# Two mixed layers in one kernel: attention released by its first block of queries instead of by the end of the projections

## The chip, the cores and the metric

The kernel runs on one core of a Trainium2 chip. The metric is device microseconds of one execution, a median over runs. One profiled execution of the kernel before is read here; it gives busy time, waits and the granted clock of every engine. TensorE (PE in the rows) does the matmuls, VectorE (DVE) and ScalarE (ACT) read their results and prepare operands, GpSimd (POOL) takes a part of the elementwise work, and SyncE (SP) issues nearly all transfers.

## The reference, cut to what matters

The program is two blocks, one after the other, over 512 positions of 1024 features, with 256 more positions of context in the first. The change touches only the two layers of the first block. In each of them one projection of the normalised input feeds three mixers, whose outputs are joined and projected back:

```python
ux = hx @ w_in[l]                      # 18 column blocks of 128
uc = hc @ (w_in[l] if ctx_out else w_in[l][:, OFF_K:OFF_HQ])
fx = fourier_mix(col(ux, OFF_FOURIER, FOURIER_W), w_four[l])
ax, ac = attention_group(ux, uc, base_c, q_norm[l], k_norm[l], tabs, ctx_out)
rx, rc = hgrn_group(ux, uc, base_c, lb_all[:, l], hg_norm[l], ctx_out)
x = x + g_a * (jnp.concatenate([fx, ax, rx], axis=-1) @ w_out[l])

def attend(q, k, v):                   # 8 heads, 2 of keys and values
    s = jnp.einsum('bkgqd,bksd->bkgqs', q, k).astype(jnp.float32) * (HEAD_DIM ** -0.5)
    p = jax.nn.softmax(s, axis=-1).astype(v.dtype)
    return jnp.einsum('bkgqs,bksd->bkgqd', p, v)
```

`hgrn_group` is a gated linear recurrence in both directions (four heads, handled as two pairs). In layer 0 context and positions both need outputs (768 columns); in layer 1 only the 512 positions do, though keys, values and the recurrence still read the context.

## The kernel before

All products of weights and activations are made of three float32r products (high by high, high by low, low by high; `mm3`, lines 245 to 247). So each weight block is fetched by a transfer on SP's queue (line 229), rounded to its high half on ACT (line 230), and its low half is made by a subtraction on DVE or POOL (line 232) before PE can use both.

Memory is handed out by two allocators written in the kernel, one for plain float32 (`arena`) and one for rounded operands (`rarena`, 440 units of 64 floats in each partition). A request takes room that was freed longest ago in a zone for short-lived buffers; a request marked long takes the lowest free room. A buffer's next owner waits for the last reader of the one before. A further 152 units (`room`) are lent to the plain allocator during the mixers.

A layer's mixers are class `Mix1`. Its work is written as generators that yield an estimated cost after each piece, and `_weave` (line 117) always continues the generator that is furthest behind, so the order of the code follows these costs. A scheduler then orders each engine's queue from that code. The generators are:

- `dense` (line 731): the projections, in the order values of the recurrence (2 blocks), its output gate (2), keys (1), attention values (1), queries (4, one block of 128 columns is two heads), Fourier inputs (2), and for the second pair of recurrence heads two gates and the queries. It ends by setting the flags `in1` and `dense`.
- `hgrn(0)` and `hgrn(1)` (line 826): the recurrence of a pair of heads. The first can start at once, the second when `in1` is set. Per step it makes state tiles `sn` (line 905).
- `attention` (line 962): for each of the four query blocks `j` and its two heads, scores (line 992), a row softmax over 768 keys (lines 562 to 571, with the exponential on ACT, line 568), the transposition of the normalised probabilities by a matmul with a diagonal (line 1004), their split into two halves (lines 212 and 213), and the product with the values (lines 1008 and 1009). It begins when `dense` is set.
- `fourier` (line 1022): also begins when `dense` is set; it follows `hgrn(1)` in its chain.
- in layer 0, `mod_cols`: products for later modulation vectors (line 498 on DVE, with a transfer of `w_ada` for each).

The gates of the recurrence use ACT's sigmoid (`zgate`, lines 640 and 641); attention uses its exponential. After the mixers come the output projection and the next phase (first additions at line 1107).

## Time and profile before

| | |
|---|---|
| median of 3 runs | 3878.45 us (3872.4 to 3878.79) |
| profiled execution, its own time | 3877.54 us |
| span of its profile | 3875.8 us |
| PE busy over the span | 3704.2 us, 96% |
| mean granted TensorE clock | 0.976 |
| layer 0: from the first query block's end to the last projection | 190 to 264 us |
| layer 0: attention | 264 to 510 us |
| layer 1: the same two stretches | 1266 to 1324 us, and 1324 to 1500 us |

A line on waits gives who waited, for whom, the total, the number of waits and the longest. A line on windows gives, for a stretch, the busy time of each engine (a union of its instructions) with the number of instructions in brackets. PE's busy time holds matmuls that overlap in the pipeline, so a share of 100% is not the peak rate, but a share below it is time in which PE had nothing running. The clock column is 1.00 at 2.4 GHz and 0.50 at 1.2 GHz, averaged over the stretch.

### The profile page before, as it was taken

The numbers are of one execution on the slowest core, as the hardware profiler recorded it, in microseconds if no ns is written. First come the engines' busy times: TensorE is split into PE (matmuls) and PEld (weight loads), VectorE is DVE, ScalarE is ACT, GpSimd is POOL, SyncE is SP. The second block draws the span as 40 slices with busy tenths as digits, with TensorE's granted clock in tenths as the row PEclk, the third lists the DMA queues.
The fourth block names the chain that finished last, engine by engine and source line by source line (L and its number), as shares of the span: only waits on it lengthen the run. The fifth ranks groups of instructions, "written<-read, shape, count | busy, mean of one in ns | idle before, by whom it ended". The sixth has DMA issues, their size and how long they took to land. (4 is left out here: it accounts for less than half of the span.)

```text
span 3875.8 us, 50567 instructions
## 1 busy us (share of the span) xinstructions
PE 3704.2 (96%) x20474; PEld 3203.6 (83%) x20474; DVE 1975.8 (51%) x3638; ACT 1345.3 (35%) x2263; POOL 591.6 (15%) x539
## 2 busy tenths in 40 slices
PE   6998899999999988999999998999999999999998
PEld 5776788888887778888988896798888888888887
DVE  8687756443254666333542358653236333736233
ACT  4233544431232354322332335443223222324222
POOL 3331012540013421000100021020002000211001
PEclk8998999999998999999999999999999999999999
DMA  5222115452202112322122321123222222312222
GB/s 208 66 93 67 39 40 181 144 181 92 61 33 74 39 65 71 103 94 91 66 95 92 110 75 51 55 90 102 81 98 98 98 75 95 109 66 98 98 94 75
DMA packets 95834, 345.12 MB, mean 89 GB/s; under 512 B 10864, under 2 KB 14064, under 8 KB 95600
## 3 DMA queue, kind: packets, MB, share of 16 engines
q1 hardware_dynamic: 95024, 341.37, 26.6%
q8 instruction: 160, 2.62, 0.3%
q14 instruction: 74, 0.61, 0.0%
q10 hardware_dynamic: 576, 0.52, 0.0%
HBM read 334.51 MB, written 4.19 MB: 87 GB/s over the span
## 5 line engine op out<-in xcount | busy, mean ns | idle before, releaser
L245 PE MATMUL psum<-rarena,room 128*128 128x512 f32 (+1 forms) x3121 | 1092.9, 351 | 5.1 <-ACT rarena L212 2.6
L247 PE MATMUL psum<-rarena,room 128*128 128x512 f32 (+1 forms) x3053 | 1076.4, 353 | 0.8 <-DVE room L232 0.8
L246 PE MATMUL psum<-rarena,room 128*128 128x512 f32 (+1 forms) x3065 | 1074.9, 351 | 0.5 <-DVE rarena L213 0.5
L247 PE MATMUL psum<-rarena 128*128 128x512 f32 (+1 forms) x2108 | 744.7, 354 | 9.9 <-DVE rarena L232 9.5
L245 PE MATMUL psum<-rarena 128*128 128x512 f32 (+1 forms) x2040 | 735.1, 361 | 16.2 <-ACT rarena L212 5.8
L246 PE MATMUL psum<-rarena 128*128 128x512 f32 (+1 forms) x2008 | 720.0, 359 | 1.3 <-DVE rarena L213 1.3
L245 PEld LDWEIGHTS psum<-rarena,room 128*128 128x128 f32 x3121 | 592.8, 190 | 82.5 <-ACT rarena L212 3.0
L246 PEld LDWEIGHTS psum<-rarena,room 128*128 128x128 f32 x3065 | 582.4, 190 | 76.0 <-DVE rarena L213 0.8
L247 PEld LDWEIGHTS psum<-rarena,room 128*128 128x128 f32 x3053 | 580.0, 190 | 78.7 <-DVE room L232 1.0
L232 DVE TENSOR_TENSOR room<-arena,room 128x1024 fp32r<-128x1024 f32 (+2 forms) x250 | 325.3, 1306 | 531.9 <-PE psum L246 231.5
L230 ACT ACTIVATE room<-arena 128x1024 fp32r<-128x1024 f32 (+2 forms) x290 | 320.1, 1110 | 738.0 <-DMA arena<-gu 242.1
L299 POOL TENSOR_TENSOR arena<-arena 128x256 f32<-128x256 f32 x170 | 136.5, 810 | 2282.8 <-ACT arena L297 2212.9
L247 PEld LDWEIGHTS psum<-rarena 128*128 128x128 f32 x2108 | 403.1, 191 | 64.2 <-DVE rarena L232 10.4
L245 PEld LDWEIGHTS psum<-rarena 128*128 128x128 f32 x2040 | 391.6, 192 | 75.5 <-ACT rarena L230 6.9
L246 PEld LDWEIGHTS psum<-rarena 128*128 128x128 f32 x2008 | 385.7, 192 | 54.6 <-DVE rarena L213 1.7
L230 ACT ACTIVATE rarena<-arena 128x1024 fp32r<-128x1024 f32 (+2 forms) x138 | 154.7, 1122 | 334.3 <-DMA arena<-gu 123.6
L232 DVE TENSOR_TENSOR rarena<-arena,rarena 128x1024 fp32r<-128x1024 f32 (+2 forms) x98 | 131.4, 1342 | 235.5 <-ACT rarena L230 114.9
L212 ACT ACTIVATE rarena<-arena 128x512 fp32r<-128x512 f32 (+2 forms) x257 | 131.2, 528 | 206.2 <-DVE arena L410 179.5
L213 DVE TENSOR_TENSOR rarena<-arena,rarena 128x512 fp32r<-128x512 f32 (+1 forms) x246 | 149.3, 622 | 87.9 <-ACT rarena L212 87.6
L297 ACT ACTIVATE arena<-arena 128x256 f32<-128x256 f32 (+1 forms) x274 | 106.9, 412 | 239.2 <-DVE arena L1230 117.3
L410 DVE TENSOR_TENSOR arena<-arena,psum 128x512 f32<-128x512 f32 (+1 forms) x170 | 100.5, 598 | 157.2 <-PE psum L247 150.9
L500 POOL TENSOR_TENSOR arena<-arena 128x1024 f32<-128x1024 f32 x48 | 125.4, 2619 | 199.9 <-DMA arena<-w_ada 88.9
(391 smaller groups left out, 4327.8 us busy)
## 6 DMA issues: line engine op xcount, KB each, us to landing
arena<-gu SPq DMA_DIRECT2D x264, 512.0 KB, 3.7
arena<-dn SPq DMA_DIRECT2D x80, 704.0 KB, 4.1
arena<-w_ada SPq DMA_DIRECT2D x60, 512.0 KB, 3.4
room<-w_ada SPq DMA_DIRECT2D x36, 512.0 KB, 4.0
room<-w_in SPq DMA_DIRECT2D x30, 512.0 KB, 3.3
arena<-c_in SPq DMA_DIRECT2D x24, 512.0 KB, 3.2
arena<-dn SPq DMA_DIRECT2D x16, 448.0 KB, 3.4
room<-ab_in SPq DMA_DIRECT2D x14, 512.0 KB, 3.2
```

Of the source, the lines that this page charges most:

```text
L212: A.activation(h, src, AF.Copy)
L213: eng.tensor_tensor(lo, src, h.bitcast(F32), ALU.subtract)
L230: A.activation(h.r, r.f, AF.Copy)
L232: (G if wlo[1] < wlo[0] else V).tensor_tensor(lo.r, r.f, h.f, ALU.subtract)
L245: PE.matmul(ps, h[:, s], ah, start=k == 0, stop=False)
L246: PE.matmul(ps, h[:, s], al_, start=False, stop=False)
L247: PE.matmul(ps, lo[:, s], ah, start=False, stop=k == nk - 1)
L297: A.activation(sq.f, src, AF.Square)
L299: (V if self.fast else G).tensor_tensor(self.parts[0].f, self.parts[0].f, sq.f, ALU.add)
L410: V.tensor_tensor(s.f, s.f, pu, ALU.mult)
L500: G.tensor_tensor(t.f, r.f, sic[q].f, ALU.mult)
```

## The change

Each query block sets a flag of its own in `dense` as soon as it has been projected, normalised and rotated. `attention` starts when the first query block's flag is set (`FIRSTQ` names block 0 for both layers), and at each further block waits for that block's flag. Nothing is computed that was not computed before. The state tiles of the recurrence become long allocations, that is, they are taken from the low end of the plain memory and no longer from the zone for short-lived buffers.

```diff
                     self.qf.append(qf)
                     self.rq.append(r8)
+                    flags.add(f"q{j}")
                     yield costq
...
-                        sn = al(128)
+                        sn = al(128, True)
                         G.memset(sn.f, 0.0)
...
-                while "dense" not in flags:
+                while f"q{FIRSTQ[l]}" not in flags:
                     yield None
...
                 for j in range(4):
+                    while f"q{j}" not in flags:
+                        yield None
                     ao = al(W, True)
...
+FIRSTQ = (0, 0)
```

By the costs that the generators yield, attention now runs from the end of the first query block. In layer 0 it has done 2.3 of its four blocks when `dense` ends, and the rest beside `hgrn(1)` and `fourier`; before, it did 2.1 blocks beside those two and 1.9 alone. In layer 1 it has done 2.3 blocks at the end of `dense` and the rest beside `hgrn(1)`; `fourier`, which had attention beside it, comes after it, and one block that attention did alone at the end is no longer there.

How that stands in the queues is shown at two places. Line numbers of the changed file are one higher after line 804 and three higher in `attention`: scores are L995 there, the transposition L1007, the products with the values L1011 and L1012. The first place is PE's queue in layer 0 where the query blocks are projected. Before, the three products of a block follow each other with only the small sums of squares (L727) between:

```order
L247 MATMUL psum<-rarena 128x512
L245 MATMUL psum<-rarena 128x512
L246 MATMUL psum<-rarena 128x512
L247 MATMUL psum<-rarena 128x512
L245 MATMUL psum<-rarena 128x512
L246 MATMUL psum<-rarena 128x512
L727 MATMUL psum<-hs,room 128x2 x2
L247 MATMUL psum<-rarena 128x512
```

Now, between the second and third query block, the first head's transpositions, value products and the next scores stand in it:

```order
L1007 MATMUL psum<-arena,room 128x128
L1007 MATMUL psum<-room 128x128 x2
L727 MATMUL psum<-hs,room 128x2 x4
L1011 MATMUL psum<-rarena 128x512
L1007 MATMUL psum<-room 128x128
L1007 MATMUL psum<-arena,room 128x128
L1007 MATMUL psum<-room 128x128 x2
L1012 MATMUL psum<-rarena 128x512
L1011 MATMUL psum<-rarena 128x512
L995 MATMUL psum<-rarena 128x256 x2
```

What moved is attention's work, from behind the last projection to between the projections.

The second place is ACT's queue in layer 1, at the gates of the second pair of recurrence heads. Before, the sigmoids stand together, and the one load of a function table before the first exponential comes after them:

```order
L641 ACTIVATE arena<-psum 128x256
L640 ACTIVATE arena<-psum 128x512
L641 ACTIVATE arena<-psum 128x512
L976 ACTIVATE rarena<-arena 64x512 x2
L854 ACTIVATE room<-arena 128x256
L819 ACTIVATE arena<-psum 128x512
L854 ACTIVATE room<-arena 128x128x2 x2
L866 ACTIVATE room<-psum 128x512
L568 ACT_TABLE_LOAD
```

Now exponentials stand between them, and so does the rounding of the next weight block (L230):

```order
L230 ACTIVATE rarena<-room 128x1024
L577 ACTIVATE arena<-psum 64x512
L568 ACT_TABLE_LOAD
L568 ACTIVATE room<-psum,room,arena 128x768 x2
L855 ACTIVATE arena<-arena 128x256
L640 ACT_TABLE_LOAD
L640 ACTIVATE arena<-psum 128x256
L641 ACTIVATE arena<-psum 128x256
L568 ACT_TABLE_LOAD
L568 ACTIVATE room<-psum,room,arena 128x768 x2
L640 ACT_TABLE_LOAD
```

In the whole program the table loads at L640 go from 2 to 7 and those at L568 from 3 to 8.

## Rows read from the trace of the kernel before

**Rows 1.** The page: busy time and share of each engine, and PE's busy tenths by slice.
```profile
PE 3704.2 (96%) x20474; PEld 3203.6 (83%) x20474; DVE 1975.8 (51%) x3638; ACT 1345.3 (35%) x2263; POOL 591.6 (15%) x539
PE   6998899999999988999999998999999999999998
```

**Rows 2.** Windows: length, then busy us (instructions) of five engines, clock, DMA share, GB/s.
```profile
190.00:264.00 74.00, 68.72 (x405) 60.89 (x406) 58.02 (x127) 20.48 (x36) 22.17 (x12) 0.96 0.32 110
264.00:380.00 116.00, 93.31 (x590) 76.32 (x588) 92.56 (x212) 50.48 (x108) 30.86 (x29) 0.90 0.19 58
430.00:512.00 82.00, 70.57 (x443) 59.77 (x442) 58.57 (x137) 49.13 (x97) 4.31 (x3) 1.00 0.16 49
1266.00:1324.00 58.00, 53.62 (x264) 44.86 (x263) 37.56 (x90) 17.82 (x29) 23.04 (x18) 0.94 0.14 47
1324.00:1410.00 86.00, 76.23 (x468) 63.55 (x467) 56.74 (x120) 41.22 (x86) 31.06 (x42) 0.90 0.08 26
1410.00:1460.00 50.00, 46.84 (x276) 40.03 (x275) 36.24 (x75) 29.59 (x52) 8.70 (x9) 1.00 0.28 91
1460.00:1505.00 45.00, 38.76 (x214) 33.08 (x213) 26.86 (x49) 24.46 (x41) 4.84 (x8) 0.92 0.22 70
2400.00:2550.00 150.00, 140.96 (x764) 115.04 (x762) 96.40 (x265) 68.94 (x159) 19.19 (x20) 0.97 0.19 62
```

**Rows 3.** Timelines (start, us): first query block rotated; last projection, then attention's first instruction.
```profile
190.34 1.26 POOL L549 TENSOR_TENSOR arena<-room 128x512 f32<-128x512 f32 x1 [2.82 <-DVE arena L275]
263.98 0.39 ACT L819 ACTIVATE arena<-psum 128x256 f32<-128x256 f32 x1 [1.18 <-PE psum L247]
264.45 3.46 ACT L976 ACTIVATE rarena<-arena 64x768 fp32r<-64x768 f32 x4
...
1266.37 1.30 POOL L549 TENSOR_TENSOR arena<-room 128x512 f32<-128x512 f32 x1
1324.54 0.60 ACT L819 ACTIVATE arena<-psum 128x512 f32<-128x512 f32 x1 [2.72 <-PE psum L247]
```

**Rows 4.** PE's waits in 430 to 512 us: total, times, longest.
```profile
PE psum L992 <- DVE arena L578: 3.9, 4, 1.6
PE psum L1004 <- ACT room L568: 3.1, 4, 1.0
PE psum L1008 <- ACT rarena L212: 1.2, 3, 0.7
PE psum L1009 <- DVE rarena L213: 0.9, 1, 0.9
```

**Rows 5.** PE's groups in 190 to 264 us: count, busy, mean ns, idle before.
```profile
L247 PE MATMUL psum<-rarena 128*128 128x256 f32 (+1 forms) x120 | 40.0, 336 | 0.6 <-DVE rarena L232 0.6
L286 PE MATMUL psum<-ident,room 128*128 128x128 f32 x6 | 1.6, 447 | 4.2 <-DVE room L284 4.2
```

**Rows 6.** ACT's timeline at a table load, at the start of layer 1.
```profile
1141.50 1.62 ACT L212 ACTIVATE rarena<-arena 128x256 fp32r<-128x256 f32 x5
1143.14 1.28 ACT L640 ACT_TABLE_LOAD   x1
1144.43 0.39 ACT L640 ACTIVATE arena<-psum 128x256 f32<-128x256 f32 x1
```

**Rows 7.** Halves of a weight block: ACT in 190 to 264, DVE in 430 to 512, POOL in 1266 to 1324.
```profile
L230 ACT ACTIVATE rarena<-room 128x1024 fp32r<-128x1024 f32 x5 | 5.3, 1060 | 23.2 <-DMA room<-w_in 16.7 <-DVE room L498 6.5
L230 ACT ACTIVATE rarena<-arena 128x1024 fp32r<-128x1024 f32 x3 | 3.2, 1060 | 14.0 <-DMA arena<-w_in 14.0
...
L232 DVE TENSOR_TENSOR rarena<-room,rarena 128x1024 fp32r<-128x1024 f32 x3 | 3.6, 1217 | 0.0
...
L232 POOL TENSOR_TENSOR rarena<-room,rarena 128x1024 fp32r<-128x1024 f32 x2 | 4.8, 2410 | 8.5 <-issue 8.5
```

**Rows 8.** SP's waits in 185 to 264 us, before transfers.
```profile
SPq L493 <- DVE room L498: 10.1, 2, 8.1
SPq L229 <- DVE room L498: 7.4, 2, 5.5
```

**Rows 9.** PE's groups of the Fourier mixer in 1410 to 1460 us.
```profile
L1067 PE MATMUL psum<-rarena 128*128 128x512 f32 x48 | 12.2, 396 | 0.0
L1050 PE MATMUL psum<-rarena 128*128 128x512 f32 x24 | 6.9, 408 | 0.0
L1035 PE MATMUL psum<-room 128*128 128x256 f32 x8 | 2.1, 379 | 0.0
```

## The prediction

> **What bounds the kernel now.** The page comes first: PE is busy 96% of the span and no other engine more than 51% [rows 1], so time can only be gained where PE has nothing running or is granted its lower clock. The windows then show where that is [rows 2]. The change can act only between the end of the first query block of a layer and the end of its mixers, that is from 190 us (the block's rotation on POOL) to 512 us, and from 1266 to 1505 us [rows 3].
>
> Four windows of these two stretches matter. Two hold the remaining projections without attention: 190 to 264 (PE busy 68.72 of 74 us) and 1266 to 1324 (53.62 of 58). Two hold the end of attention with nothing beside it but the first weights of the output projection: 430 to 512 (70.57 of 82) and 1460 to 1505 (38.76 of 45) [rows 2]. The reader should see two different limits in them. In the projections PE waits for weights for only 0.6 us, and most of its idle time is one wait of 4.2 us [rows 5]. In the end of attention PE waits in short pieces along one head's chain: scores wait for the last head's output on DVE, transpositions for the exponential on ACT, value products for the two halves on ACT and DVE [rows 4]. There DVE is busy 58.57 us of 82 and ACT 49.13 [rows 2]; no engine is full, the chain is only too short of independent work.
>
> **The change part by part.** It adds and removes no arithmetic. Attention's four blocks are equal work, so what the order shows (2.3 blocks beside the projections, the rest beside the recurrence) amounts to this: the lonely ends of attention are laid beside the remaining projections. *The term:* the four windows together are 74 + 82 + 58 + 45 = 259 us, with PE busy 68.72 + 70.57 + 53.62 + 38.76 = 231.67, or 89.4%. The joint stretches need 231.67 us divided by the share of PE that the mixture reaches. For that share the trace has near rows. The best one is the second block's mixer at 2400 to 2550 us: there, too, projections are woven with a softmax attention that starts block by block, and PE is busy 140.96 of 150 us, 94.0% [rows 2]. At 94.0% the stretches take 246.5 us, a gain of 12.5. The lower end is the recurrence with attention, 264 to 380 and 1324 to 1410 us: 169.54 of 202, 83.9% [rows 2], which gives 276.1, a loss of 17.1. The upper end is PE without a gap: 231.7, a gain of 27.3. I take 94.0%, because the kind of work and the load beside it agree: DVE in the joint stretches would be busy 58.02 + 58.57 + 37.56 + 26.86 = 181 us of 246, 74%, where that mixer has 96.40 of 150, 64% [rows 2]. It is not the same, so two deductions follow.
>
> *Table loads.* Sigmoids and exponentials now alternate, which puts ten more table loads into ACT's queue. One takes 1.28 us, and the next activation starts 1.29 us after the load began [rows 6], so this is 12.8 us of ACT. ACT's work in the joint stretches is 20.48 + 49.13 + 17.82 + 24.46 = 112 us of 246 [rows 2], so it has room; but each load stands ahead of an exponential or of a gate for which PE will wait. Hidden entirely it costs 0, exposed entirely 12.8; I take 2, near the lower end, since the neighbouring matmuls of a projection run on meanwhile. The Trainium skill, "ScalarE: Activation LUTs", section "What ACT_TABLE_LOAD costs", adds a drain of about 1.38 us to each load, 2.66 us for a switch; ten would be 26.6 us of ACT. The trace does not show that drain around a load [rows 6], so the sum keeps the measured figure.
>
> *Weights.* By the sizes in the code, at the last projections of layer 0 the rounded memory has 104 of its 440 units free before (192 are activations, 24 the first head pair's output, 48 keys, 24 values, 48 Fourier inputs); a weight block's two halves take 32, so three blocks can be in hand. Now a finished query block's output (24) and the current head pair's queries (24) are held as well, which leaves 56: one weight block and one pair of split probabilities (16). So the next block can only be rounded after the last has been read. Where nothing else covers it, that is 1.06 us on ACT and 1.22 on DVE, or 2.41 on POOL [rows 7]: 2.3 to 3.5 us for each of sixteen projections (eight in each layer, from the second query block on). PE's order puts pieces of attention between projections, which covers most; I take 3 us in all, a little more than one projection of the sixteen fully exposed. The bounds are 0 and 16 × 2.3 = 37, of which the 83.9% row already includes waits of this kind.
>
> *Behind a waiting instruction.* ACT works in order, and in 190 to 264 us it stood before weight roundings for 30.7 us until a transfer landed and 6.5 until DVE [rows 7], since SP's transfers of weights stood behind those of the modulation vectors, which wait for DVE (10.1 and 7.4 us) [rows 8]. Nothing hung on that before. Now exponentials and splits of attention queue behind those roundings. The stretch is twice as long for the same transfers, so I price this at nothing in the sum and keep it as a reason for the slow side.
>
> *Fourier in layer 1* loses the attention beside it (1410 to 1460 us, PE 93.7% busy [rows 2]). Its matmuls, 12.2 + 6.9 + 2.1 = 21.2 us, waited for nothing [rows 9]; at 83.9% instead of 93.7% they would take 2.6 us more. I take 0 and keep 2.6 as a bound. *The state tiles* change only addresses; POOL, which clears them, is idle for 52 us of the 74 [rows 2]: 0.
>
> *Sum.* −12.5 + 2 + 3 = −7.5 us. From the profiled execution's own 3877.54 us (span 3875.8) that is 3870.0. The median of the runs shown, 3878.45, lies 0.9 above the profiled execution, so against it the forecast is 8.4 us or 0.22% faster. About 0.2%, 7.8 us, is what a measurement of this kernel can tell from no change.
>
> **The rivals.** *Nothing left over:* the mixture reaches only the 89.4% that the four windows have now, and the chains merely trade places; 259 us stay 259 and the time is about 3877. For it: the four windows lie between 86% and 93%, and nothing in the mechanism removes a wait of attention's own chain. Against it: the 94.0% row. That the change does not do what it says belongs here too, but the order already shows attention between the projections.
>
> *Memory becomes the limit (slower):* with room for one weight block, each projection waits for its rounding, ACT stands before it, attention's splits stand behind it on ACT, and PE, which also works in order, runs out of both. The place is every projection after the second query block, the price at 83.9% is 17.1 us, 3894.6, with Fourier's 2.6 3897. It decides once the share of PE in the joint stretch falls below 89.4%. For it speak the 30.7 us that ACT waited for transfers [rows 7] and that the second block's mixer, from which I took 94.0%, is not short of memory; against it, that the order covers the gaps with attention. In the Trainium skill, "Perfetto Trace Analysis", section "Identifying the Most-Contended Engine", repeated equal gaps on the engine that should be full are named as a possible sign that there is not enough memory for the next tile. By that rule this rival would show as one gap of 2 to 3 us per projection; the trace of before has no such pattern in its projections [rows 5], the memory being wider there.
>
> *Full packing:* both kinds of work fill each other's gaps entirely, 27.3 us less, and about 3852 after the table loads. The projections run at 93% with no help, so it is not excluded.
>
> **How the numbers follow.** The forecast, a gain that survives its two deductions (3855 to 3870.5), gets 0.33; full packing 0.07; nothing left over 0.31; memory as the limit 0.29. So faster by over 0.2% has 0.40, within 0.2% 0.31, slower 0.29. The predicted time is the forecast's, 3870. For 8 in 10 the range must reach into the slow rival as well: from the full packing without deductions, 3850, to 3898, the slow rival with Fourier's bound.
>
> **What would show it right or wrong.** The first scores should run soon after 190 and 1266 us, and no longer only with the last projection at 264 and 1324 [rows 3]. In the joint stretches, about 190 to 338 and 1266 to 1364 us if the forecast holds, PE should be busy 94% or more; under 89.4% the gain is gone. PE's waits of line 245 to 247 for the roundings (230 and 232), 0.6 us in the first window before, should stay under 5 us in all; over 15 would be the memory rival. Table loads should number 25 instead of 15, at 1.28 us. Layer 0 should end about 6 us earlier and layer 1 gain only 2 more, since its memory is as narrow and its Fourier mixer stands alone. If the first layer gains nothing although its projections are filled, the step on ACT's order was priced wrongly.

## The result: 1.2% slower, and over a quarter of it in a stage that was not changed

The changed kernel takes 3920.83 us (median of 4 runs, 3916.66 to 3933.61), the kernel before 3875.97 beside it (3872.4 to 3878.79): a ratio of 1.0116, 95% interval 1.0099 to 1.0132, or 45 us more. In the profiled executions the spans are 3914.6 and 3875.8 us, 38.8 apart. Engine line of the page of after, to be held against [rows 1]:

```profile
PE 3721.8 (95%) x20474; PEld 3213.1 (82%) x20474; DVE 1967.5 (50%) x3638; ACT 1361.0 (35%) x2273; POOL 585.7 (15%) x539
```

PE has the same 20474 matmuls, but is busy 17.6 us longer; ACT has ten instructions more, the table loads. Where the 38.8 us arise can be read from ACT's table loads, since those at lines 409 (first activation of each layer's feed-forward), 1417 (1420 in after; gates of the second block's mixer) and 407 (the feed-forward behind that mixer) stand at fixed places of the program. From ACT's rows of these lines (number of loads, their shortest, median and longest ns, first and last start in us); before, then after:

```profile
L409 ACT ACT_TABLE_LOAD  x2: 1283/1283/1283, 565.7 to 1547.9; - x2
L1417 ACT ACT_TABLE_LOAD  x1: 1283/1283/1283, 2343.4 to 2343.4; - x1
L407 ACT ACT_TABLE_LOAD  x1: 1283/1283/1283, 2577.8 to 2577.8; - x1
```

```profile
L409 ACT ACT_TABLE_LOAD  x2: 1283/1283/1283, 583.5 to 1574.4; - x2
L1420 ACT ACT_TABLE_LOAD  x1: 1283/1283/1283, 2371.1 to 2371.1; - x1
L407 ACT ACT_TABLE_LOAD  x1: 1283/1283/1283, 2616.8 to 2616.8; - x1
```

The differences of these starts are the lengths of five stages. The same reading is given for the experiments (us more or less than before, one profiled execution each):

| kernel | to layer 0's feed-forward | to layer 1's | to the mixer's gates | mixer | rest |
|---|---|---|---|---|---|
| before (us) | 565.7 | 982.2 | 795.5 | 234.4 | 1298.0 |
| after | +17.8 | +8.7 | +1.2 | +11.3 | −0.2 |
| sn_long | +10.7 | −6.0 | −3.3 | −0.5 | −0.7 |
| early_l0 | +19.3 | +5.7 | −2.5 | +5.5 | −1.8 |
| early_l1 | +10.8 | +10.9 | −3.5 | +6.5 | −0.6 |
| early_l0_pin | +25.1 | +4.9 | −4.3 | 0.0 | −0.4 |
| bank_turn | +14.8 | −3.3 | +2.1 | +3.7 | −0.3 |
| after_turn | +13.6 | +7.6 | +2.5 | +14.4 | −0.2 |
| early_l1_q2 | +9.3 | −3.4 | −0.4 | +4.5 | −0.4 |

Of the 38.8 us, 17.8 are lost in layer 0 (5.1 of them ahead of the first query block, which is rotated at 195.4 us instead of 190.3), 8.7 up to layer 1's feed-forward, and 11.3 in the second block's mixer, of which the diff touches no line. One execution is good to some 5 us in a stage: up to layer 0's feed-forward early_l0 and early_l0_pin have the same order, and differ by 5.8. Some traces are further off: bank_turn's is the longest of its ten runs, 10.6 us above their median, and those of mods_off and after_packed are 15 and 13 us above theirs.

The first attention instructions and the last projections, from the timelines of POOL and ACT of after (start, us), answer [rows 3]:

```profile
195.39 2.08 POOL L549 TENSOR_TENSOR arena<-room 128x512 f32<-128x512 f32 x1 [1.41 <-DVE room L548]
197.51 1.71 ACT L979 ACTIVATE rarena<-arena 64x768 fp32r<-64x768 f32 x2 [2.23 <-POOL arena L549]
354.14 0.38 ACT L820 ACTIVATE arena<-psum 128x256 f32<-128x256 f32 x1 [1.68 <-PE psum L247]
...
1284.11 1.28 ACT L979 ACTIVATE rarena<-arena 64x512 fp32r<-64x512 f32 x2 [3.96 <-POOL arena L549]
1404.25 0.60 ACT L820 ACTIVATE arena<-psum 128x512 f32<-128x512 f32 x1
```

So the change does what it says. Windows (columns as in [rows 2]) of before: layer 0 from the first rotation to the feed-forward, from there to layer 1's feed-forward, the mixer:

```profile
190.30:565.70 375.40, 329.81 (x2037) 283.63 (x2038) 267.67 (x608) 161.11 (x322) 70.60 (x55) 0.95 0.19 61
565.70:1547.90 982.20, 938.47 (x5563) 825.57 (x5562) 512.95 (x964) 366.62 (x663) 254.17 (x202) 0.97 0.29 93
2343.40:2577.80 234.40, 214.42 (x1151) 176.16 (x1150) 166.72 (x414) 117.08 (x246) 46.26 (x46) 0.93 0.16 55
```

Windows of after: the same three, then the two joint stretches and the first 18 us of attention:

```profile
195.40:583.50 388.10, 341.26 (x2028) 293.22 (x2029) 255.61 (x595) 167.17 (x324) 70.08 (x56) 0.90 0.18 61
583.50:1574.40 990.90, 939.26 (x5563) 823.86 (x5562) 510.41 (x966) 373.86 (x668) 249.88 (x202) 0.97 0.28 92
2371.10:2616.80 245.70, 215.35 (x1142) 175.41 (x1141) 167.62 (x413) 115.92 (x244) 45.89 (x46) 0.92 0.16 53
195.40:354.00 158.60, 132.32 (x766) 116.02 (x767) 100.66 (x249) 71.04 (x131) 24.20 (x14) 0.89 0.16 54
1284.00:1404.00 120.00, 110.58 (x603) 91.12 (x602) 75.30 (x172) 64.73 (x108) 32.28 (x34) 0.96 0.08 27
195.40:213.20 17.80, 5.20 (x16) 4.17 (x17) 14.98 (x31) 5.72 (x7) 4.45 (x2) 0.60 0.35 118
```

Length less busy time is PE's idle time. In layer 0 it was 45.6 us and is 46.8: the interleaving took nothing from it. PE's busy time rose by 11.5, at a mean granted clock of 0.90 instead of 0.95. From there to layer 1's feed-forward the idle time rose from 43.7 to 51.6 and the busy time by 0.8. In the mixer the idle time rose from 20.0 to 30.4 and the busy time by 0.9. PE's largest waits in layer 0 (us in all, times, longest), before in 190 to 566 us, then after in 195 to 584, there with the two for the halves of a weight block:

```profile
PE psum L992 <- DVE arena L578: 5.0, 5, 1.6
PE psum L863 <- DVE room L841: 4.7, 1, 4.7
PE psum L286 <- DVE room L284: 4.2, 1, 4.2
PE psum L1009 <- DVE rarena L213: 3.9, 4, 2.2
PE psum L1004 <- ACT room L568: 3.6, 5, 1.0
```

```profile
PE psum L995 <- ACT room L568: 10.3, 5, 7.6
PE psum L995 <- DVE rarena L980: 7.0, 1, 7.0
PE psum L1012 <- DVE rarena L213: 5.5, 6, 1.4
PE psum L995 <- DVE arena L578: 4.1, 3, 2.0
PE psum L245 <- ACT rarena L230: 1.8, 3, 0.9
PE psum L247 <- DVE rarena L232: 0.5, 1, 0.5
```

Many short waits on one head's chain became few long ones: 7.0 for the first query's low half and 7.6 for the first exponential, both in the first 18 us of attention, where PE works 5.2 us.

### The profile page after: what moved, and what is told of

The parts are those of the page before. It is cut to its first block, busy times and chain, and to the rows that moved or that the text cites. A ratio compares the mean times of both kernels' runs of the same rounds, so it can differ in the third digit from the quotient of the medians.

```text
span 3914.6 us, 50605 instructions
## 1 busy us (share of the span) xinstructions
PE 3721.8 (95%) x20474; PEld 3213.1 (82%) x20474; DVE 1967.5 (50%) x3638; ACT 1361.0 (35%) x2273; POOL 585.7 (15%) x539
## 5 line engine op out<-in xcount | busy, mean ns | idle before, releaser
L247 PEld LDWEIGHTS psum<-rarena,room 128*128 128x128 f32 x3062 | 581.7, 190 | 83.9 <-DVE room L232 4.0
L232 DVE TENSOR_TENSOR room<-arena,room 128x1024 fp32r<-128x1024 f32 (+2 forms) x257 | 339.4, 1325 | 585.5 <-ACT room L230 275.5
L230 ACT ACTIVATE room<-arena 128x1024 fp32r<-128x1024 f32 (+2 forms) x292 | 322.0, 1109 | 685.9 <-DMA arena<-gu 243.4
L230 ACT ACTIVATE rarena<-arena 128x1024 fp32r<-128x1024 f32 (+2 forms) x139 | 155.6, 1122 | 328.2 <-DMA arena<-gu 85.0
L232 DVE TENSOR_TENSOR rarena<-arena,rarena 128x1024 fp32r<-128x1024 f32 (+2 forms) x105 | 139.5, 1329 | 230.5 <-ACT rarena L230 117.0
L213 DVE TENSOR_TENSOR rarena<-arena,rarena 128x512 fp32r<-128x512 f32 (+2 forms) x248 | 140.8, 585 | 81.4 <-ACT rarena L212 81.1
```

Of the source, the lines that this page charges most:

```text
L213: eng.tensor_tensor(lo, src, h.bitcast(F32), ALU.subtract)
L230: A.activation(h.r, r.f, AF.Copy)
L232: (G if wlo[1] < wlo[0] else V).tensor_tensor(lo.r, r.f, h.f, ALU.subtract)
L247: PE.matmul(ps, lo[:, s], ah, start=False, stop=k == nk - 1)
```

## Experiments

Theory A: attention beside the projections is itself the loss. B: the state tiles' place is. C: much of it is an accident, another order of the queues that any small change sets off. Ratios are to the kernel before on the same chip, with 95% intervals.

**The state tiles.** One word, in both layers (sn_long), or in layer 1 alone (state_l1); and after without it (sn_short).

```diff
-                        sn = al(128)
+                        sn = al(128, True)      # sn_long
+                        sn = al(128, last)      # state_l1
```

> The kernel before with the long allocation of the recurrence's state tiles alone; attention still waits for all projections. The profile of the changed kernel is 5 us late already when the first query block is rotated (195.4 against 190.3 us), ahead of any attention. Theory A (attention beside the projections lowers PE's share; the tiles' place costs only those 5 us): 3876 to 3882, 0 to +6. Theory B (most of the loss comes from the tiles' place, through addresses and the waits on them): 3895 or more, +20 or more. If the 5 us have another cause (the scheduler's order), the time is that of before, 3873 to 3879, and the first query block is rotated at 190.

3882.36 us, ratio 1.0014 (1.0004 to 1.0025): A's bound, +6. The profiled execution shows 10.7 lost in layer 0 and won back later; 4.2 of them come ahead of the first query block (rotated at 194.5 us instead of 190.3). Behind it the weights of the next projections, those of the second and third query block, come late. SP's timeline in 176 to 203 us shows them issued at 187.8 and 193.5 in before, and in sn_long behind two transfers of modulation weights (line 493), for which SP waited 10.5 us until DVE's broadcast copies left a buffer; PE then waited 9.2 us. Over the whole of layer 0, though, PE's idle time is 46.1 us, as before (45.6), and its busy time 335.8 instead of 329.8, so this wait is not shown to be the loss. Before, then sn_long, with SP's wait in 176 to 215 and PE's in 185 to 215:

```profile
187.82 0.33 SPq L229 DMA_DIRECT2D room<-w_in  x1
193.51 0.33 SPq L229 DMA_DIRECT2D arena<-w_in  x1
```

```profile
185.62 11.32 SPq L493 DMA_DIRECT2D room<-w_ada  x2
201.93 0.80 SPq L229 DMA_DIRECT2D room<-w_in  x2
...
SPq L493 <- DVE room L284: 10.5, 1, 10.5
...
PE psum L245 <- ACT rarena L230: 9.2, 1, 9.2
```

> The kernel before with the long allocation of the state tiles in layer 1 alone; attention waits for all projections. With it in both layers, layer 0 lost 10.7 us and layer 1 won 10.4 back. Up to layer 1 the order is that of before, from there on that of the run with both. If the two are independent, as the orders say: 3866 to 3868, 0.2 to 0.3% under the kernel before, with the win between 1150 and 1425 us. If layer 1 only made up for a disturbance that layer 0 had left: 3875 to 3880.

3875.49, ratio 1.0004 (0.9995 to 1.0013): the second case. Layer 1 has nothing of its own to win by the tiles' place; what it won in sn_long goes with the delay in layer 0 ahead of it.

> The changed kernel with the state tiles allocated as before, so that only the early start of attention is left. Theory A: the changed kernel's 3920.8 less 0 to 6, so 3914 to 3921. Theory B: 3880 to 3900. If both parts matter only together, it is between.

3933.59, ratio 1.0140 (1.0119 to 1.0161): neither. With the early start the long place helps by some 9 (by the ratios) to 13 us (by the medians), though the intervals touch. So B falls.

**One layer at a time.** The wait at the head of attention takes its flag by layer (in early_l1_q2 that of the third block); the state tiles are long in both layers:

```diff
-FIRSTQ = (0, 0)
+FIRSTQ = ("q0", "dense")     # early_l0
+FIRSTQ = ("dense", "q0")     # early_l1
+FIRSTQ = ("dense", "q2")     # early_l1_q2
-                while f"q{FIRSTQ[l]}" not in flags:
+                while FIRSTQ[l] not in flags:
```

> The changed kernel, with the early start in layer 0 alone; layer 1 waits for all projections, as before. By the profile of the changed kernel layer 0 lost some 18 us in all, 5 of them ahead of attention, layer 1 10 to 12, and the second block's mixer 12, which the change doesn't touch. Theory A, with each layer's loss its own: 3876 + 18 = 3894 at the end of layer 0's feed-forward, 3894 in all if the mixer's 12 us go with layer 1's change, 3906 if they go with layer 0's. Theory C (the mixer's loss comes from the order or addresses that are left over, and may fall either way): layer 0's +18 stays, and the mixer's 12 appear in both, in one or in none of the two runs with one layer early.

3905.23, ratio 1.0073 (1.0058 to 1.0088).

> The changed kernel, with the early start in layer 1 alone (state tiles long in both layers). Theory A: layer 0 ends at most 5 us late; layer 1 loses 10 to 12, so 3886 to 3893 without the mixer's 12 us, 3898 to 3905 with them. Theory B: layer 0 loses most of its 18 us here too, from the state tiles. Sum rule: if the two layers' losses are independent, the excess over 3876 of this run and of the one with layer 0 early add up to the changed kernel's 45, counting the 5 us of the state tiles once.

3907.35, ratio 1.0076 (1.0061 to 1.0092). Counting the tiles' 6 us once, the two excesses make 29 + 31 − 6 = 54, more than 45, so they are not independent. Against sn_long, early_l0 loses 8.6 us in layer 0 and then 11.7 up to layer 1's feed-forward, where its attention is not early; early_l1 loses 16.9 there. Both lose 6 to 7 us in the mixer against sn_long, as C has it.

> The kernel with only layer 1 early, started at its third query block instead of its first; state tiles long in both layers. With the first block it took 3907, 25 us more than with the state tiles alone (3882): some 15 of them in layer 1 and 9 in the second block's mixer. If the loss in layer 1 grows with the time that attention stands beside projections: 5 to 10 us in layer 1, total 3890 to 3902. If it is a matter of starting early at all: 3902 to 3912.

3884.65, ratio 1.0025 (1.0016 to 1.0035), lower than either case: against sn_long layer 1 loses 2.6 us instead of 16.9. But it is no test of a later start, as the expectation has it. The flag moves attention in the text of the program; the scheduler still puts the first scores as early. PE's first scores in layer 1, in early_l1 and in early_l1_q2:

```profile
1282.64 3.33 PE L995 MATMUL psum<-rarena 128*128 128x512 f32 x10 [1.56 <-DVE rarena L980]
```

```profile
1281.82 1.33 PE L995 MATMUL psum<-rarena 128*128 128x512 f32 x8
```

Of layer 1's 128 score matmuls 70 run before the last projection in early_l1, 57 here, 1 in sn_long. So attention beside the projections need not lose in layer 1, and A falls there: it is the order in which the two are mixed. Windows of layer 1 up to the feed-forward, in sn_long, early_l1 and early_l1_q2:

```profile
1114.60:1552.60 438.00, 400.25 (x2464) 348.99 (x2463) 274.86 (x638) 185.95 (x365) 115.09 (x142) 0.95 0.17 58
```

```profile
1115.80:1569.60 453.80, 411.33 (x2461) 355.74 (x2461) 267.99 (x638) 191.98 (x369) 115.53 (x142) 0.92 0.17 56
```

```profile
1112.00:1553.80 441.80, 401.73 (x2442) 350.23 (x2441) 268.78 (x624) 190.32 (x368) 114.16 (x142) 0.93 0.17 57
```

Idle time is 37.8, 42.5 and 40.1 us, busy time 400.3, 411.3 and 401.7: two thirds of early_l1's loss is busy time at a lower granted clock, and the other mixture, with 22 matmuls fewer in its window, has almost none of it.

**Accidents of order.** The banks' order turned at the start, in before and in after; and in early_l0 the mixer's queues pinned to the order of before by edges that order issue and wait for nothing.

```diff
+        banks.freed[:8] = [0, -1, -2, -3, -4, -5, -6, -7]   # bank_turn, after_turn
```

```diff
+        traced = list(nc.cur_bb.bb.instructions)[at["mix2_0"]:at["outp0"]]   # early_l0_pin
+        for e, o in QUEUE.items():
+            q = [i for i in traced if str(i.engine) == f"EngineType.{e}" ...]
+            for a, b in zip(o, o[1:]):
+                tc.add_manual_dep(q[b], q[a].name, nosync, reason="order of before")
```

> The kernel before with nothing changed but the order in which the eight PSUM banks are first handed out: 7 6 5 4 3 2 1 0 instead of 0 to 7. Attention still waits for all projections; work, memory and tile sizes are those of before. The scheduler makes another order of it in some stretches, and in the second block's mixer the same one as in the run with only layer 0 early, where that mixer took 5.5 us longer than before. Theory C (an order that differs by accident is what costs there): the mixer (from its first gate activation to its output, 168.5 us before) takes 173 to 175 us with no early attention at all, with one wait of 7 us or more for a softmax sum, and the layers may move by up to 10 us each way. Theory A (early attention costs): the mixer takes 168 to 170 us and the total is 3873 to 3880.

3883.94, ratio 1.0021 (1.0009 to 1.0033).

> The kernel with only layer 0 early, and all five queues of the second block's mixer put into the order of the kernel before (ordering edges without waits). Its addresses in that mixer are those of before but for the PSUM banks' names. Theory C: the mixer falls from 174 to 168 or 169 us, and the total from 3905 to about 3900. Rival (the loss there comes from something else that the early start leaves behind, such as the banks or the state of the chip): the mixer stays at 174 us and the total at 3905. All before the mixer stays as in the run with layer 0 early: +22 us at its start.

3903.97, ratio 1.0083 (1.0070 to 1.0096). The median fell by 1.3 us only, less than the interval; the stage shows it. The mixer takes 234.4 us before, 239.9 in early_l0, 238.1 in bank_turn without any early attention, and 234.4 in early_l0_pin. PE's longest waits in the mixer, in after, early_l0 and bank_turn, then in early_l0_pin and before (against before, bank_turn's lines stand one further down, early_l0_pin's four, and after's three):

```profile
PE psum L1481 <- DVE room L569: 7.7, 1, 7.7
```

```profile
PE psum L1481 <- DVE room L569: 7.6, 1, 7.6
```

```profile
PE psum L1479 <- DVE room L570: 7.6, 1, 7.6
```

```profile
PE psum L251 <- DVE rarena L236: 5.2, 1, 5.2
```

```profile
PE psum L247 <- DVE rarena L232: 5.1, 1, 5.1
PE psum L245 <- ACT rarena L230: 3.7, 2, 2.1
```

The wait of 7.6 us, transpositions for the reciprocal of a softmax sum, comes with the other order and goes with it. That the order costs in this mixer is shown, both ways, for early_l0; in after, whose rounded tiles lie elsewhere, the same wait stands, but its queues were not pinned. The other traces agree. Compared instruction by instruction, up to a few at the ends, six have the mixer in the order of before (before, sn_long, state_l1, before_copy, and the two that are pinned): 231.4 to 234.4 us. Three have early_l0's order (with early_l1_q2 and bank_turn): 238.1 to 239.9. Two have after's (with after_copy): 245.7 and 247.7.

> The changed kernel with nothing else changed but the order in which the eight PSUM banks are first handed out, the same turn that cost the kernel before 8 us. If the loss of 45 us belongs to the early start, the time stays between 3905 and 3935, that is 3920 with an accident of 10 to 15 us each way. If it was mostly an accident of order, a turn can give much of it back: under 3900.

3917.19, ratio 1.0102 (1.0085 to 1.0118): the early start keeps most of its loss when the order is shaken.

**Table loads.**

```diff
-                A.activation(dd[:, o], p, AF.Sigmoid)
-                A.activation(km[:, o], p, AF.Sigmoid, scale=-1.0)
+                A.activation(dd[:, o], p, AF.Copy if b else AF.Sigmoid, scale=0.01 if b else 1.0)
+                A.activation(km[:, o], p, AF.Copy if b else AF.Sigmoid, scale=-0.01 if b else -1.0)
```

> The changed kernel, with the sigmoids of the second head pair's gates (lines 640 and 641, in both layers) computed as scaled copies, which need no table: a part of the computation is changed, and the ten table loads that the early start added are gone; PE's, DVE's, POOL's and SP's orders are unchanged. Theory T (the loads stand on the path): 10 to 13 us less than the changed kernel, 3908 to 3911. The forecast's price was 2 us: 3917 to 3920.

3922.65, ratio 1.0121 (1.0108 to 1.0135): no gain, with 15 table loads as in before.

> The control: the same replacement (lines 640 and 641, the second head pair's gates as scaled copies) in the kernel before, where these sigmoids stand among other sigmoids and no table load goes away. Expected 3873 to 3878, no change, so that a difference in the changed kernel is the loads' own.

3876.25, ratio 1.0000 (0.9991 to 1.0009). Ten loads, 12.8 us of ACT, cost nothing that can be measured: the intervals of the changed kernel with and without them, some 6 us each way, leave no room for theory T's 10 to 13 us, but would for the forecast's 2. By the Trainium skill, "ScalarE: Activation LUTs", section "What ACT_TABLE_LOAD costs", with its 2.66 us for a switch, ten would be an estimated 26.6 us of ACT; the rows show 1.28 us for a load and no drain around it [rows 6].

**The standstill at attention's start.** Layer 0's modulation sums moved from DVE to POOL and ACT (mods_off); their transfers from SP's queue to POOL's (after_modq, before_modq); and the flag of layer 0's third block (from_q2_l0).

```diff
-MODV = ((0, 1, 2, 3), (2,))
+MODV = ((), (2,))            # mods_off
-MODQ = 0
+MODQ = 1                     # after_modq, before_modq
-FIRSTQ = (0, 0)
-TEMPS = ((180, 220),) * 10
+FIRSTQ = (2, 0)              # from_q2_l0
+TEMPS = ((180, 200),) + ((180, 220),) * 9
```

> The changed kernel with layer 0's modulation vectors multiplied on POOL and summed on ACT instead of both on DVE. In the changed kernel PE stands for about 14 of the first 19 us of attention (194 to 213), while DVE is busy all the time, four of these 1.2 us sums among its work, and the granted clock is 0.69. Theory D (DVE, not memory, is what the mixture lacks in layer 0): the joint stretch 195 to 354 gets 5 to 12 us shorter and PE's idle time at its start falls under 8 us; total 3909 to 3916. Rival (PE's own order: attention's first scores stand ahead of the next projection, whatever DVE does): the stretch moves by less than 3 us. Second rival: POOL and ACT, which now carry the sums, become late, and the stretch gets longer.

3942.45, ratio 1.0180 (1.0161 to 1.0199): the second rival's outcome; that POOL and ACT came late was not traced. The joint stretch grew from 158.6 to 174.4 us and PE was idle for 12.2 of the first 18, with DVE's sums gone. (The clock that is quoted for 194 to 213 us of the changed kernel should read 0.59.)

> The changed kernel with the modulation weights' transfers issued from POOL's queue instead of SP's. In the changed kernel SP's queue stood from 182.6 to 191.5 us and again to 196.4 us at two such transfers, which waited for a buffer that DVE's broadcast copies held; the third query block's weights, behind them, were issued at 198.2 (before: 187.8 and 193.5), rounded at 202.2, and PE stood for 14.6 of the first 18 us of attention. Theory E (SP's order is what starves PE there, in the run with the state tiles alone too, where PE waited 9.2 us for that rounding): those weights are rounded by 197, PE's idle time from 195 to 213 falls from 12.6 to under 5 us, and layer 0 ends 8 to 14 us earlier; total 3906 to 3914. Rival F (attention's first scores stand ahead of the projection on PE, and wait for the query's halves and for the exponential whatever SP does): PE's idle time there stays over 10 us and the total moves by less than 5 us, or gets longer where POOL's queue makes the vectors late.

(The block that it calls the third is the second.) 3933.22, ratio 1.0144 (1.0128 to 1.0160). PE was idle for 11.3 of the first 18 us, in two waits of 7.3 us for the first query's low half and for the exponential, as in after. That is F's outcome. It is no test of E, since the weights were issued no earlier, at 202.1; SP's wait in 178 to 225 us shows why:

```profile
SPq L229 <- POOL arena L549: 26.3, 1, 26.3
```

With the modulation transfers gone, the weights themselves waited for the buffer of the query block's rotation on POOL. It is memory, but neither the rounded memory nor the place that the prediction spoke of: the buffer into which a block lands.

> The control: the kernel before with the modulation weights' transfers issued from POOL's queue. Its weights were in time there (rounded at 191.2, 196.8, 200.5), so by theory E it gains nothing in layer 0: 0 to +5 us at the first feed-forward. Its order in the second block's mixer is, by the program, the one that cost 6 us with the banks turned; so 3876 to 3890. If it gains as much as the changed kernel does, POOL's queue is better for another reason.

3888.70, ratio 1.0032 (1.0020 to 1.0043): inside the expected range, though the first feed-forward comes 11.3 us later and not 0 to 5. POOL's queue is no better place in general.

> The changed kernel, with attention in layer 0 started when the third query block is ready (35 to 40 us later than in the changed kernel), and in layer 1 with the first as there; 20 units of the rounded memory are moved from the short-lived to the long-lived side in this phase, without which it doesn't fit. Theory E or F (a standstill at the start, while the weights come late): by then the weights have caught up, so PE's idle time in the first 18 us of attention falls under 5 us and layer 0 ends 8 us or more earlier than in the changed kernel. Theory A (the mixture itself runs at a lower granted clock for as long as it lasts): layer 0 wins only in proportion, under 5 us. Total by the first 3905 to 3913, by the second 3914 to 3921.

3943.18, ratio 1.0174 (1.0160 to 1.0187), more than any case. Four score matmuls ran at 195.4 us (the first at 200.4 in after), but the next at 224.0 and the first exponential at 229.4 (211.5 in after), so here attention did start later. From 224 to 242 us PE was idle for 4.3 us, under the 5 of E and F; yet layer 0 ended 11.3 us later than in after, and not 8 earlier. So most of the standstill at the start, where E and F look for the loss, went (PE waited 6.9 us for a weight block ahead of it) without giving the time back. With the other division of the rounded memory this is one more order: up to the feed-forward PE's idle time is 49.7 us and its busy time 354.1 instead of 341.3, at a granted clock of 0.88, and 22 us more than in before are lost on the way to layer 1's feed-forward. Windows from the first rotation, and of 224 to 242 us:

```profile
191.00:594.80 403.80, 354.13 (x2048) 304.46 (x2049) 256.63 (x605) 166.95 (x326) 65.33 (x56) 0.88 0.17 59
224.00:242.00 18.00, 13.74 (x73) 12.48 (x71) 12.90 (x43) 7.81 (x14) 2.53 (x2) 0.81 0.09 30
```

**PSUM banks.** Scores of two query tiles in three banks instead of four, released as a pair:

```diff
-                                spb = ps(nk)
-                                sp = spb.f
+                                o = qt % 2 * nk
+                                if not o:
+                                    spb = ps(2 * nk)
+                                sp = spb.f[:, o:o + nk]
...
-                                pf_(spb)
+                                if o:
+                                    pf_(spb)
```

> The changed kernel with the scores of two query tiles packed into three PSUM banks instead of four, in both layers: four tiles then take six banks of eight, released by pairs. Theory P (banks are what the mixture lacks): PE's waits at the scores' line in layer 0, 14.4 us for the exponential and the head's output, fall under 7 us, PE's idle time in layer 0 from 46.8 us to under 40, and the total by 8 to 20 us to 3900 to 3913. Rival (in-order PE with one head's chain, whatever the banks): the idle time stays within 5 us, and the total within an accident of 10 to 15 us of 3920; since banks are released only by pairs, it may also get longer.

3948.50, ratio 1.0179 (1.0161 to 1.0198). PE's waits at the scores for the exponential and the head's output, 14.4 us in after, are 21.1, and its idle time in layer 0 is 64.7 us.

> The control: the kernel before with the same packing. There attention stands beside the recurrence alone, whose tiles need one bank each. Theory P: it gains less than the changed kernel does, 0 to 6 us against 8 to 20. By the program its second block's mixer stands in the order that cost 6 us, so 3872 to 3885.

3920.23, ratio 1.0113 (1.0098 to 1.0128). P's gain did not come: both got slower, before by 44 us, after by 28. The packing releases banks later, but it also cuts the score matmuls differently and changes the order, so which of these costs is not shown. A form that needs fewer banks and releases them as early was not tried, so whether the mixture is short of banks stays open.

**What is left to win.** Layer 0 as before, layer 1 as in early_l1_q2, the mixer pinned:

> Layer 0 as before (state tiles short, attention after all projections), layer 1 early from its third query block with its state tiles long, and the queues of the second block's mixer in the order of before. By the stages of the run with layer 1 early from the third block (9 us lost in layer 0, 3 won in layer 1, 4.5 lost in the mixer): 3870 to 3876. If the 3 us in layer 1 were only layer 0's loss handed back, as with the state tiles alone: 3875 to 3880, and nothing is left to win.

3874.08, ratio 0.9989 (0.9979 to 0.9999): in the first of the two ranges, but a tenth of a per cent, less than a measurement tells from no change. In its trace layer 1 wins 2.3 us, while layer 0 and the mixer, which have before's order, differ from before by +4.2 and −3.0, so the 2.3 are no more than scatter. With the accidents taken away, attention beside the projections of layer 1 is worth next to nothing, which is the rival *Nothing left over* for that layer. No version here beats the kernel before by more.

## Why the prediction was wrong, step by step

**What bounds the kernel** was right as far as it went: PE. But its busy time was taken for a fixed 231.67 us, to be divided by a share. It is not fixed: over layer 0 it rose by 11.5 us with nearly the same matmuls (2028 and 2037), at a granted clock of 0.90 instead of 0.95.

**The term −12.5 failed.** The mixture was to reach the 94.0% of the second block's mixer, and the joint stretches to take 246.5 us. They reached 83.4% (158.6 us) and 92.2% (120 us), together 87.2% and 278.6 us, in layer 0 the very row, 83.9%, that I named as the lower end and gave to the slow rival. PE's idle time, the only thing that interleaving can take away, rose by 1.2 us in layer 0 and 7.9 up to layer 1's feed-forward. The 94.0% row left out its own stage's beginning: from 2343 to 2400 us PE is busy 47.15 of 56.6 us, 83.3%, and waits 5.1 us for the low half of a weight block and 2.1 for the high one (rows of before above). A stretch in which such a mixture has settled was taken for one in which it starts. And the order was taken as given by the change, while early_l1_q2 mixes the same work with 14 us less than early_l1 up to layer 1's feed-forward.

**Table loads, +2:** 25 instead of 15 as announced; no cost measured, within some 6 us. **Weights, +3:** right in size. PE's waits for the roundings at lines 245 and 247 in the joint stretches are 1.4 and 3.0 us, together under the 5 announced, so the memory rival's sign did not come. The Trainium skill ("Perfetto Trace Analysis", section "Optimization Strategy", not the one that the prediction gives) names one gap that keeps repeating as a possible sign of too little memory. No such row came here: PE's two long gaps, of 7.0 and 7.6 us, are single ones.

**Behind a waiting instruction, 0:** wrong, and announced as a reason for the slow side; but it was DVE's queue and PE's own, more than ACT's. PE stood for 12.6 of attention's first 17.8 us. At first, up to 200.4 us, it had nothing ready: the first query's halves were only being made, and the next block's weights, issued at 198.2 us instead of 187.8 since their buffers were held, were not rounded. From 205.0 to 212.6 the weights were there, their low half from 205.7 on. But in PE's queue the last of the first scores stood ahead of the projection and waited for the exponential, and ACT, which had waited 3.0 us for the weights' transfer, stood 6.9 us until DVE came to the input of that exponential (L567), behind two modulation sums and other work. Yet this standstill is not shown to be the loss: in from_q2_l0 PE idles 4.3 us at that place, and layer 0 is longer still. From the timelines of after:

```profile
203.34 2.38 POOL L232 TENSOR_TENSOR rarena<-room,rarena 128x1024 fp32r<-128x1024 f32 x1 [5.86 <-PE psum L995]
210.20 1.28 ACT L568 ACT_TABLE_LOAD   x1 [6.94 <-DVE arena L567]
212.63 0.80 PE L995 MATMUL psum<-rarena 128*128 128x256 f32 x2 [7.62 <-ACT room L568]
```

**The state tiles, "only addresses: 0":** +6 us by themselves. Addresses bring other waits: in sn_long SP waited 10.5 us for a buffer ahead of the weights.

**What had no term:** the stages behind. The second block's mixer lost 11.3 us in after without a changed line; in early_l0 the 5.5 that it lost are shown to be the order of its queues, and after's own order came with 245.7 and 247.7 us in its two traces. What the order costs in layer 1 is open, since nothing was pinned there.

**The signs.** Layer 0 was to end 6 us earlier and ended 17.8 later, "although its projections are filled", which I had put down in advance to the step on ACT's order; in the first 18 us the trace shows DVE's and PE's queues in its place. The slow rival's direction came true; its mechanism, one gap per projection, did not, and 3897 was too little since it had neither the clock nor the mixer. The range's end, 3898, was therefore 19 us short of the lowest run.

**What the traces add, and what stays open.** Four traces have layer 0 in the order of before (before, state_l1, l1_q2_pin, before_copy) and four in that of after (after, early_l0, early_l0_pin, after_copy, the last but for its gates). From the first rotation to the feed-forward the first four take 374.8 to 379.1 us, with 329.8 to 335.8 busy, the others 388.1 to 395.0, with 340.1 to 344.6 busy. So the loss in layer 0 repeats with the order. On average it is 14.6 us there, 9.0 of busy time (the clock is 0.90 to 0.91 instead of 0.93 to 0.95) and 5.6 of idle time. Why the mixture's order has the lower clock stays open. It doesn't take early attention: bank_turn has 0.91, in one long execution, and sn_long's 335.8 us busy at 0.93 are no more than state_l1 has with before's order. Nor is the idle time the same however attention is laid: it is 40.4 to 51.5 us in these eight, 53.2 in sn_short, 55.4 in after_modq, 62.5 in mods_off and 64.7 in after_packed. Windows of layer 0 in state_l1, early_l0_pin and bank_turn:

```profile
191.60:567.80 376.20, 335.83 (x2037) 289.47 (x2038) 264.59 (x609) 161.80 (x322) 69.47 (x55) 0.93 0.18 61
195.80:590.80 395.00, 344.64 (x2029) 296.01 (x2030) 255.76 (x595) 167.20 (x325) 71.15 (x56) 0.90 0.18 60
192.30:580.50 388.20, 343.56 (x2037) 295.67 (x2038) 263.54 (x608) 161.59 (x322) 70.36 (x55) 0.91 0.18 59
```

## What to carry to other kernels

Before filling an engine's gaps with other work, ask whether that work's inputs are there at that moment, and count the engine's idle time and its busy time apart: interleaving can only take from the first, and here a lower granted clock added to the second. In a kernel whose order a scheduler makes, any change reorders stages far away (a turn of the PSUM banks alone cost 8 us), and a flag in the text need not be a time on the chip: put such a change beside a neutral one, and compare untouched stages, before the difference is credited to the idea.

## What the runs showed of the chip

The granted clock does not follow the share of busy time alone. From 430 to 512 us before PE is busy 86% and is granted 1.00 [rows 2], with no wait over 1.6 us [rows 4]; in the joint stretch of layer 0 after it is busy 83% and is granted 0.89, and 0.60 in the first 17.8 us, near the lower of the two levels (1.2 of 2.4 GHz), where it had stood still for 7.0 and 7.6 us at a time. Over layer 0 about the same idle time (46.8 us for 45.6) in fewer, longer pieces came with a lower clock, 0.90 for 0.95. At the start this repeats: the four traces with after's order, where PE stands for 12.3 to 13.0 of the first 18 us, have 0.59 to 0.63 there, and the four with before's, where it stands for 3.2 to 3.4, have 0.72 to 0.83. Long standstills are not all of it: bank_turn, with 3.2 us there and no wait over 4.9 us in layer 0, still has 0.91.
